# Orders of all engines from a list scheduler inside the kernel: a two-layer retention and attention trunk on one core

## The chip, the core and the metric

The kernel runs on one core of one Trainium2 chip. The metric is the device time of one execution in microseconds (us); lower is better. Below, PE is the matrix engine (TensorE), DVE the vector engine, ACT the scalar engine, POOL GpSimd, and SP the engine that issues most transfers (SyncE). Each engine works through its own list of instructions strictly in order; between engines there are only semaphores. So whatever stands late in one engine's list is late, even if its inputs have long been there.

## The reference, cut to what matters

A residual stream of 256 tokens by 2048 features goes through one retention layer and one latent-attention layer, each followed by a squared-ReLU MLP, all in float32:

```
x = x + retention(rms_norm(x), w_in, w_out, cos, sin)      # 8 heads, 2 chunks of 128 tokens
x = x + square(relu(rms_norm(x) @ w1[0])) @ w2[0]          # 2048 -> 8192 -> 2048
k_nope, k_pe, v = mla_shared_kv(rms_norm(x), w_kv_down, w_kv_up, ...)
x = x + mla_attention(rms_norm(x), w_dq, w_uq, w_o, k_nope, k_pe, v, cos, sin)   # 16 heads
x = x + square(relu(rms_norm(x) @ w1[1])) @ w2[1]
```

## The kernel before

**Precision and products.** Every large operand is split into a rounded high part and a low remainder: ACT writes the high part (`wh` for weights), DVE the remainder (`wl`), both in `split`. A product is three matmuls, high by high, high by low, low by high (lines 409 to 411 for most of the kernel).

**Tiling.** `gemm_pair` works through a 256-by-1024 block of weights ("quad") at a time and for some of the quads ("sevens", lists such as `SEVEN`, `ODD`, `LATE`) replaces eight block products by seven: DVE forms sums of weight blocks (`u`, lines 363, 372, 373), and sums of activation blocks were made ahead by `with_sums` (tiles named `..._more`). A plain quad costs PE 24 matmuls, a seven 21. Raw weights come into `raw` (3 buffers), split parts go to `wh` and `wl` (5 buffers each), other 2 KB tiles share `f2k` (14 buffers), activations `act` (24 buffers). PSUM has the tags `acc` (4 banks), `tp` (2) and `at` (one pair).

**Stages in order of time.** Retention: a first projection `rg`, then queries, keys and values (`rq`, `rk`, `rv`, `rp`) head by head, with short score and value products (`sc`, `o`) whose results `y` are transposed on PE and split; out-projection `ro`. MLP of layer 0: up-projections `u` and down-projections `d` alternate in four groups; hidden blocks are transposed on PE, squared and split into `hid` tiles. Then the new `x` is normed and transposed (`n_tp`) into `n` tiles; the key side `kd`, the query side `dqp`, `dq`; `ku`, `uq`; attention (`s`, `ptp`, `ao`) between pieces of `uq` and `wo`; the second MLP; stores.

**What sets the order.** The Python code decides it. `later(n, fn)` puts work off by a number of half-chunks of the weight stream, `tick` runs what is due, and the engines' lists follow the order of the calls as the framework schedules them. At some places `queued_behind` adds a dependency without a semaphore, to hold an instruction behind another one on its engine. Buffers of a tag are handed out in turn.

Of the kernel before, what the change touches and what calls it, by code (L numbers as in the profile page):

```python
# [14 lines left out]
I32 = mybir.dt.int32  # L15
AF = mybir.ActivationFunctionType
# [3 lines left out]


# [24 lines left out]
GROUPS = (4, 4, 4, 4)  # L46
SEVEN, LATE, ODD, HEAD = (3, 5, 7), (5, 7), (1, 3, 5, 7), (2, 4, 6, 7)
# [19 lines left out]
def yoco(ctx: ExitStack, tc: tile.TileContext, a):  # L67
    nc = tc.nc
# [3 lines left out]
    def f2k(shape, name, dtype=F32):  # L72
        return pool.tile([P, *shape], dtype, tag="f2k", bufs=14, name=name)

    def small(w, name):
        return pool.tile([P, w], F32, tag="small", bufs=36, name=name)
# [5 lines left out]
    def bank(tag, shape, name):  # L82
        t = psum.tile([P, 512], F32, tag=tag, bufs=4 if tag == "acc" else 2, name=name)
        return shaped(t, shape)

    def two_banks(name):
        return psum.tile([P, 2, 512], F32, tag="at", bufs=1, name=name)

    def act_tile(name, dtype=F32R):

        return pool.tile([P, 2, 2, S], dtype, tag="act", bufs=24, name=name)


    queue, low_part, first_low = [], [None], [None]
    clock, count, ahead = [0], itertools.count(), [None, None]
# [19 lines left out]
    gains = pool.tile([P, G_ALL], F32, name="gains")  # L115
    cst = pool.tile([P, C_ALL], F32, name="cst")
    pos_i = pool.tile([P, NT], I32, name="pos_i")
    gpe = pool.tile([P, 2 * ROPE], F32, name="gpe")
# [3 lines left out]
    neg_half = pool.tile([P, 16], F32, name="neg_half")  # L122
# [4 lines left out]
    zeros = pool.tile([P, 512], BF16, tag="junk", bufs=1, name="zeros")  # L127
# [6 lines left out]
    x_home = [[dram.tile([P, 512], F32, name=f"xh_{t}_{b}") for b in range(NB)] for t in range(NT)]  # L134
# [14 lines left out]
    def to_home(c, p):  # L149

        def send(t, j, i):
            ins = nc.gpsimd.dma_start(x_home[t][2 * p + j], c[t][j][i], accum_op=ALU.add)
            tc.add_manual_dep(
                ins.ins, low_part[0].ins.name,
                mybir.DependencyInfo(mybir.DependencyClass.Sync, mybir.DependencyReason.SCHED_ONLY), reason="spaced",
            )
# [8 lines left out]
    def sums_into_x(c, name):  # L165
# [6 lines left out]
        queued_behind(nc.vector.tensor_tensor(v, c["p6"], o["p1"], op=ALU.add), low_part[0])  # L172
        nc.vector.tensor_tensor(u, c["p7"], v, op=ALU.add)

        def join(*parts):
            for t, j, part, op in parts:
                queued_behind(nc.vector.tensor_tensor(x[t][j], x[t][j], part, op=op), low_part[0])
# [31 lines left out]
    def square_sum(src, acc, name):  # L209
        junk = pool.tile([P, 512], BF16, tag="junk", bufs=1, name=f"{name}_sq")  # L210
# [26 lines left out]

    def stream(w, chunk, cols, name, use, done=None, before=None):

        raw = pool.tile([P, 2048], F32, tag="raw", bufs=3, name=f"{name}_raw")  # L240
# [3 lines left out]
        for half in range(2):  # L244
            wh = pool.tile([P, 1024], F32R, tag="wh", bufs=5, name=f"{name}_wh{half}")
            wl = pool.tile([P, 1024], F32R, tag="wl", bufs=5, name=f"{name}_wl{half}")
# [10 lines left out]
            for i in range(cuts):  # L257
                lo = half * n + i * m
                low_part[0] = split(wh[:, i * m : (i + 1) * m], wl[:, i * m : (i + 1) * m], raw[:, lo : lo + m])
                if ahead[0] is not None:  # L260
                    queued_behind(low_part[0], ahead[0])
                    ahead[0] = None
# [52 lines left out]
    def queued_behind(ins, before):  # L315
        tc.add_manual_dep(
            ins.ins, before.ins.name,
            mybir.DependencyInfo(mybir.DependencyClass.NoSync, mybir.DependencyReason.DATA), reason="order",
        )

    def quad(w, chunk, x, mm, name, split_ends=False):

        raw = pool.tile([P, 2048], F32, tag="raw", bufs=3, name=f"{name}_raw")
# [9 lines left out]
        def parts(src, n, part, after=None):  # L333
            wh = pool.tile([P, 1024], F32R, tag="wh", bufs=5, name=f"{name}_wh{part}")
            wl = pool.tile([P, 1024], F32R, tag="wl", bufs=5, name=f"{name}_wl{part}")
            low = low_part[0] = split(wh[:, : n * 512], wl[:, : n * 512], src)
            if after is not None:
                queued_behind(low, after)
            if part == 0:
                first_low[0] = low  # L340
# [21 lines left out]
        u = [pool.tile([P, 2, 512], F32, tag="us", bufs=2, name=f"{name}_u{i}") for i in range(2)]  # L362
        first_sum = nc.vector.tensor_tensor(
# [3 lines left out]
        if first_low[0] is not None:  # L367
            queued_behind(first_sum, first_low[0])
        if ahead[1] is not None:
            queued_behind(first_sum, ahead[1])  # L370
            ahead[1] = None
        nc.vector.tensor_tensor(u[1][:, 0], u[0][:, 0], raw[:, 512:1024], op=ALU.add)
        summed_up = nc.vector.tensor_tensor(u[1][:, 1], u[1][:, 0], raw[:, 1536:], op=ALU.add)  # L373
        b11, b22 = parts(raw[:, 0:1024], 2, 0, summed_up)
        mm("p1", a(0, 0), b11)
        mm("c12", s(3), b22)
        (b21,) = parts(raw[:, 1536:], 1, 1, summed_up)
# [156 lines left out]
    def add_to_x(acc, b, ss, name):  # L534
        for t in range(NT):
            for part in acc[t] if isinstance(acc[t], tuple) else (acc[t],):
                added = nc.vector.tensor_tensor(x[t][b], part, x[t][b], op=ALU.add)
                if name == "n2" and b >= 2:
                    queued_behind(added, low_part[0])
# [19 lines left out]
    pos_f = pool.tile([P, NT], F32, name="pos_f")  # L559
# [733 lines left out]
```

## Time and profile before

| | |
|---|---|
| time, median of 3 runs | 2460.17 us (2459.62 to 2461.29) |
| span of the profiled execution, first to last instruction | 2456.3 us |
| median less span (the profiled execution's own total is not listed) | 3.9 us |
| busy share PE / PE weight loads / DVE / ACT / POOL | 100 / 84 / 90 / 67 / 10 % |
| granted TensorE clock | 1.000 |
| DMA mean | 212 GB/s |

A row of a timeline gives the start in us from the first instruction, the duration, the engine, line and operation, the tiles written and read, and in brackets the idle time before it with what ended it. A matmul's end in these rows is modelled: a 512-column matmul has 0.39 us, while its successor starts after 0.23 us. So time lost on PE is read from the distance between two starts, not from the idle time alone.

### The profile page before, as it was taken

The numbers are of one execution on the slowest core, as the hardware profiler recorded it, in microseconds if no ns is written. First come the engines' busy times: TensorE is split into PE (matmuls) and PEld (weight loads), VectorE is DVE, ScalarE is ACT, GpSimd is POOL, SyncE is SP. The second block draws the span as 40 slices with busy tenths as digits, with TensorE's granted clock in tenths as the row PEclk, the third lists the DMA queues.
The fourth block names the chain that finished last, engine by engine and source line by source line (L and its number), as shares of the span: only waits on it lengthen the run. The fifth ranks groups of instructions, "written<-read, shape, count | busy, mean of one in ns | idle before, by whom it ended". The sixth has DMA issues, their size and how long they took to land.

```text
span 2456.3 us, 31721 instructions
## 1 busy us (share of the span) xinstructions
PE 2446.2 (100%) x11614; PEld 2057.6 (84%) x11614; DVE 2212.2 (90%) x2919; ACT 1641.3 (67%) x2307; POOL 238.0 (10%) x287
## 2 busy tenths in 40 slices
PE   9999999999999999999999999999999999999999
PEld 7888888888888888888888888998888888888887
DVE  7899899888899999999999998777899999999998
ACT  6566666556676767667676777577667667676674
POOL 6400001000000010010110001101000100100100
PEclk9999999999999999999999999999999999999999
DMA  8555569556565586695786555444555865957854
GB/s 309 207 201 191 192 202 259 191 183 224 197 218 194 196 254 218 207 272 187 241 253 213 200 202 180 155 162 173 197 199 205 252 228 194 262 198 229 264 209 170
DMA packets 93692, 521.05 MB, mean 212 GB/s; under 512 B 11104, under 2 KB 12512, under 8 KB 40288
## 3 DMA queue, kind: packets, MB, share of 16 engines
q1 hardware_dynamic: 72144, 472.83, 55.2%
q0 software_dynamic: 21248, 46.15, 8.9%
q8 instruction: 91, 1.49, 0.2%
q14 instruction: 65, 0.53, 0.1%
q10 hardware_dynamic: 144, 0.05, 0.0%
HBM read 479.14 MB, written 39.85 MB: 211 GB/s over the span
## 4 chain that ended last, share of the span: by engine, by line
PE 92%; DVE 2%; ACT 1%; issue 0%; DMA 0%; POOL 0%; ACTq 0%; DVEq 0%
PE u_c L411 7%; PE u_c L410 7%; PE u_c L409 7%; PE d_c L411 6%; PE d_c L410 6%; PE d_c L409 6%; PE rp_c L411 3%; PE rp_c L409 3%; PE rp_c L410 3%; PE u_p L411 2%; PE u_p L410 2%; PE u_p L409 2%; PE rq_acc L307 2%; PE rk_acc L307 2%; PE ro_c L411 2%; PE ro_c L409 2%
## 5 line engine op out<-in xcount | busy, mean ns | idle before, releaser
L217 DVE TENSOR_TENSOR d_wl<-d_raw,d_wh 128x1024 fp32r<-128x1024 f32 (+1 forms) x256 | 278.7, 1111 | 31.6 <-ACT d_wh L216 31.6
L217 DVE TENSOR_TENSOR u_wl<-u_raw,u_wh 128x1024 fp32r<-128x1024 f32 (+1 forms) x256 | 279.3, 1113 | 29.8 <-ACT u_wh L216 29.8
L409 PE MATMUL u_c<-u_wh,n 128*128 128x512 f32 x712 | 278.3, 392 | 0.0
L411 PE MATMUL u_c<-u_wh,n 128*128 128x512 f32 x712 | 277.2, 389 | 0.0
L410 PE MATMUL u_c<-u_wl,n 128*128 128x512 f32 x712 | 277.2, 389 | 0.0
L409 PE MATMUL d_c<-d_wh,hid 128*128 128x512 f32 x706 | 275.4, 392 | 0.5 <-ACT d_wh L216 0.5
L411 PE MATMUL d_c<-d_wh,hid 128*128 128x512 f32 x706 | 275.0, 390 | 0.0
L410 PE MATMUL d_c<-d_wl,hid 128*128 128x512 f32 x706 | 274.8, 389 | 0.0
L216 ACT CAST u_wh<-u_raw 128x1024 fp32r<-128x1024 f32 (+1 forms) x256 | 241.3, 973 | 49.6 <-PE u_c L411 24.1
L216 ACT CAST d_wh<-d_raw 128x1024 fp32r<-128x1024 f32 (+1 forms) x256 | 240.3, 971 | 39.9 <-PE d_c L411 16.6
L216 ACT CAST d_wh<-d_u 128x1024 fp32r<-128x1024 f32 x106 | 108.1, 1051 | 119.7 <-DVE d_u L373 82.6
L216 ACT CAST u_wh<-u_u 128x1024 fp32r<-128x1024 f32 x104 | 106.2, 1052 | 116.0 <-DVE u_u L373 77.3
L411 PEld LDWEIGHTS u_c<-u_wh,n 128*128 128x128 f32 x712 | 133.7, 188 | 27.8
L410 PEld LDWEIGHTS u_c<-u_wl,n 128*128 128x128 f32 x712 | 133.8, 188 | 27.4 <-DVE u_wl L217 0.3
L409 PEld LDWEIGHTS u_c<-u_wh,n 128*128 128x128 f32 x712 | 133.7, 188 | 27.0
L409 PEld LDWEIGHTS d_c<-d_wh,hid 128*128 128x128 f32 x706 | 132.6, 188 | 28.2 <-ACT d_wh L216 1.4
L411 PEld LDWEIGHTS d_c<-d_wh,hid 128*128 128x128 f32 x706 | 132.5, 188 | 27.6
L410 PEld LDWEIGHTS d_c<-d_wl,hid 128*128 128x128 f32 x706 | 132.6, 188 | 27.5 <-DVE d_wl L217 0.4
L216 ACT CAST rp_wh<-rp_raw 128x1024 fp32r<-128x1024 f32 x112 | 103.8, 945 | 74.2 <-PE rp_c L411 49.2
L217 DVE TENSOR_TENSOR rp_wl<-rp_raw,rp_wh 128x1024 fp32r<-128x1024 f32 x112 | 119.7, 1090 | 16.4 <-ACT rp_wh L216 16.2
L217 DVE TENSOR_TENSOR u_wl<-u_u,u_wh 128x1024 fp32r<-128x1024 f32 x104 | 123.5, 1222 | 3.1 <-ACT u_wh L216 2.8
L217 DVE TENSOR_TENSOR d_wl<-d_u,d_wh 128x1024 fp32r<-128x1024 f32 x106 | 125.8, 1221 | 0.0
(570 smaller groups left out, 6505.3 us busy)
## 6 DMA issues: line engine op xcount, KB each, us to landing
u_raw<-in_mlp_w SPq DMA_DIRECT2D x128, 1024.0 KB, 5.4
d_raw<-in_mlp_w SPq DMA_DIRECT2D x128, 1024.0 KB, 4.9
rp_raw<-in_ret_w_gv SPq DMA_DIRECT2D x56, 1024.0 KB, 4.8
ro_raw<-in_ret_w_out SPq DMA_DIRECT2D x32, 1024.0 KB, 4.9
uq_raw<-in_mla_w_uq SPq DMA_DIRECT2D x24, 768.0 KB, 4.3
rq_raw<-in_ret_w_qk SPq DMA_DIRECT2D x16, 1024.0 KB, 4.9
rk_raw<-in_ret_w_qk SPq DMA_DIRECT2D x16, 1024.0 KB, 4.8
xh<-d_c POOLq DMA_DIRECT2D x48, 256.0 KB, 6.1
```

The lines of the kernel that those rows point to most:

```text
L216: nc.scalar.copy(h, src)
L217: return nc.vector.tensor_tensor(l, src, h.bitcast(F32), op=ALU.subtract)
L307: nc.tensor.matmul(acc[f], wh[:, cols], a.rearrange("p i s -> p (i s)"), start=k == 0, stop=k == nk - 1)
L409: nc.tensor.matmul(dst, ah, bh, start=n == 0, stop=False)
L410: nc.tensor.matmul(dst, ah, bl, start=False, stop=False)
L411: nc.tensor.matmul(dst, al, bh, start=False, stop=n == total[key] - 1)
```

## The change

All engine calls go to a `Plan` instead of the hardware queues. `record` notes each operation with the tiles it reads and writes (down to the single elements) and an estimated cost; nothing is emitted until the whole program is recorded. Then `due_dates` walks backwards and gives every operation a due time (the latest start by the costs of what follows it; PE's operations are chained in the recorded order), and `schedule` walks forward: on each engine, among the operations whose inputs and buffers are ready, the one with the earliest due time goes next. Buffers get a slot when an operation is placed, any free one, and for `f2k`, `act` and `small` not necessarily in turn. `emit` issues everything in that order, under a mode of the framework that keeps it.

With it `queued_behind` and all its uses go. Two more edits ride along: in the retention every transposed `y` block is now first copied by ACT from PSUM to SBUF and split from there (before, only the blocks that get sums; that is ten copies more), and in the MLP `with_sums` is recorded half a step after the split, which matters only to the recorded order. The code for turning blocks by DMA (`turn_by_dma`) is there but switched off by `TURNED_Y = 0` and `STEPS` of `None`. The lists of sevens are the same sets as before.

```diff
+AHEAD = {"f2k": 25000, "act": 30000, "small": 60000}
...
+class Plan:
+    LATENCY = {"PE": 55, "DVE": 36, "ACT": 48, "POOL": 110, "SP": 60}
...
+    def due_dates(self):
+        last = {}
+        for op in self.ops:
+            for other in op.before.values():
+                other.after.append((op, True))
+            if op.engine == "PE":
+                if "PE" in last:
+                    last["PE"].after.append((op, False))
+                last["PE"] = op
...
+        for op in reversed(self.ops):
+            op.due = 0.0
+            whole = op.took if op.moves is None else op.cost + sum(op.moves)
+            for other, finish in op.after:
+                gap = whole + self.LATENCY[other.engine] if finish and not (other.engine == op.engine == "PE") else op.cost
+                op.due = min(op.due, other.due - gap)
+            if not op.after:
+                op.due = -whole
...
+    def schedule(self):
...
+            best = None
+            for e in free:
+                w, r = waiting[e], ready[e]
+                while w and w[0][0] <= free[e]:
+                    _, _, op = heapq.heappop(w)
+                    heapq.heappush(r, (op.due, op.number, op))
+                at = free[e] if r else w[0][0] if w else None
+                if at is not None and (best is None or at < best[0]):
+                    best = (at, e)
...
+            op.start = at
+            free[e] = at + op.cost
+            if op.moves is None:
+                op.end = at + op.took
+            else:
+                server = max(server, at + op.cost) + op.moves[0]
+                op.end = server + op.moves[1]
...
+        order = self.schedule()
+        with self.tc.manual_schedule(engines=engines):
+            for op in order:
+                engine, method = op.method
+                fn = getattr(getattr(self.nc, engine), method)
+                op.made = fn(*(real(v) for v in op.args), **{k: real(v) for k, v in op.kw.items()})
...
-    nc = tc.nc
+    nc = Plan(tc.nc, tc)
...
-        if first_low[0] is not None:
-            queued_behind(first_sum, first_low[0])
...
+        def split_up(k2, src):
+            yt = act_tile(f"y{h}{k2}")
+            split_act(yt, src)
+            summed_up = len(y_act) in (HEAD if h < RH // 2 else LATE)
+            y_act.append((yt, with_sums(src, f"y{h}{k2}") if summed_up else None))
...
-                else:
-                    split_act(yt, tp)
+                u = f2k([2, S], f"yu{h}{k2}")
+                nc.scalar.copy(u, tp)
+                split_up(k2, u)
...
+                    if len(blocks) - 1 in ODD:
+                        later(0.5, lambda: entry.__setitem__(1, with_sums(u, name)))
```

**Three places in the engines' lists.** In the changed kernel all instructions carry line 421, the line that issues them. The order of PE is almost the one before; what moves is mostly DVE, ACT, SP and POOL.

SP, the start of the program, before (`x0t` is the transposed input, `rg_raw` the first weights, `cst` a table with the constants of the rotary angles, the mask and the identity for transposes):

```order
L648 DMA x0t_99<-in_xt 128x256
L253 DMA rg_raw<-in_ret_w_gv 128x512
L656 DMA x0t_99<-in_xt 128x256
L253 DMA rg_raw<-in_ret_w_gv 128x512 x2
...
L687 DMA pos_i<-in_pos 128x2
L688 DMA cst<-in_cst 128x672
```

SP, the same place with the change:

```order
L421 DMA cst<-in_cst 128x672
L421 DMA rg_raw<-in_ret_w_gv 128x512
L421 DMA x0t_77<-in_xt 128x256
L421 DMA rg_raw<-in_ret_w_gv 128x512
L421 DMA x0t_77<-in_xt 128x256
```

The table moves from the fourteenth place of the list to the first, ahead of all that the first matmul needs.

DVE, the end of the first MLP, before (`d_317` is the last quad of the last down-projection, `d_31_v`, `d_31_u` and `x_mlp` its sums into `x`, `kd` the first weights after it):

```order
L217 TENSOR_TENSOR d_317_wl_12571<-d_317_raw,d_317_wh_12570 128x1024
L177 TENSOR_TENSOR x_mlp_12025<-x_mlp_12025,d_31_u 128x512
L217 TENSOR_TENSOR d_317_wl_12587<-d_317_raw,d_317_wh_12586 128x1024
L177 TENSOR_TENSOR x_mlp_12106<-x_mlp_12106,d_31_p_12560 128x512 x2
L177 TENSOR_TENSOR x_mlp_12106<-x_mlp_12106,d_31_v 128x512
L177 TENSOR_TENSOR x_mlp_12106<-x_mlp_12106,d_31_u 128x512
L217 TENSOR_TENSOR kd_wl_12614<-kd_raw,kd_wh_12613 128x640
L537 TENSOR_TENSOR x_mlp_12025<-d_31_c_12209,x_mlp_12025 128x512
L537 TENSOR_TENSOR x_mlp_12025<-d_31_c_12213,x_mlp_12025 128x512
L217 TENSOR_TENSOR kd_wl_12638<-kd_raw,kd_wh_12637 128x640
```

DVE, the same place with the change:

```order
L421 TENSOR_TENSOR d_317_wl_12568<-d_317_raw,d_317_wh_12551 128x1024
L421 TENSOR_TENSOR d_317_wl_12581<-d_317_raw,d_317_wh_12557 128x1024
L421 TENSOR_TENSOR kd_wl_12590<-kd_raw,kd_wh_12565 128x640
L421 TENSOR_TENSOR kd_wl_12597<-kd_raw,kd_wh_12585 128x640
L421 TENSOR_TENSOR d_31_v<-d_31_p_12498,d_31_p_12574 128x512
L421 TENSOR_TENSOR x_mlp_11571<-x_mlp_11571,d_31_p_12574 128x512
L421 TENSOR_TENSOR d_31_u<-d_31_p_12498,d_31_v 128x512
L421 TENSOR_TENSOR kd_wl_12620<-kd_raw,kd_wh_12610 128x640
L421 TENSOR_TENSOR x_mlp_11571<-x_mlp_11571,d_31_u 128x512
L421 TENSOR_TENSOR x_mlp_11634<-x_mlp_11634,d_31_p_12578 128x512 x2
```

The remainders of the last weights, and of the first two pieces of `kd`, now stand ahead of the sums into `x`. In the last down-projection of the second MLP the same happens to its own weights.

DVE, the first down-projection of a group, before (`hid_13` is the last hidden block, `hid_13_more` its sums, `d_007` the weights of the quad that multiplies them):

```order
L217 TENSOR_TENSOR hid_13_7524<-hid_13_u,hid_13_7524 128x2x256
...
L217 TENSOR_TENSOR hid_13_more<-hid_13_sum,hid_13_more 128x2x256
...
L217 TENSOR_TENSOR d_006_wl_7712<-d_006_raw,d_006_wh_7711 128x1024
L372 TENSOR_TENSOR d_007_u_7730<-d_007_u_7729,d_007_raw 128x512
L373 TENSOR_TENSOR d_007_u_7730<-d_007_u_7730,d_007_raw 128x512
L217 TENSOR_TENSOR d_007_wl_7735<-d_007_raw,d_007_wh_7734 128x1024
```

DVE, the same place with the change:

```order
L421 TENSOR_TENSOR d_006_wl_7723<-d_006_raw,d_006_wh_7714 128x1024
L421 TENSOR_TENSOR d_007_wl_7732<-d_007_raw,d_007_wh_7720 128x1024
L421 TENSOR_TENSOR d_007_u_7705<-d_007_u_7705,d_007_raw 128x512
L421 TENSOR_TENSOR hid_13_7586<-hid_13_u,hid_13_7586 128x2x256
L421 TENSOR_TENSOR hid_13_more<-hid_13_sum,hid_13_more 128x2x256
L421 TENSOR_TENSOR d_007_wl_7754<-d_007_raw,d_007_wh_7728 128x512
```

The split of the last hidden block, and of its sums, moves from 22 and 16 rows ahead of the first remainder of `d_007` to two and three rows behind it.

More of the change, by code (lines that the diff above doesn't have):

```diff
@@ L802, in ret_valued @@
             vl = f2k([512], f"vl{h}{t}", F32R)
-            low = split(vh, vl, src[t], r0[t])
-            if ahead[0] is not None:
-                queued_behind(low, ahead[0])
+            split(vh, vl, src[t], r0[t])
             v.append((vh, vl))
@@ L895, in mlp @@
+                for i in range(2):
+                    later(TURNS[p % 2][i], lambda i=i: turn(i))
             for p in range(f0 // 2, (f0 + nf) // 2):
-                seven = SEVEN if p % 2 else ODD if p else LATE
+                seven = (ODD, SEVEN)[p % 2] if p else LATE
                 gemm_pair(
@@ L942, in yoco @@
     rc, ckv = [], []
[L943 removed]
+    kpe_t = nc.tile(pool, [P, 2, S], F32R, "kpe_t")
     def downed(acc, b):
```

524 lines of the change are left out of this document (428 added, 96 removed).

## The prediction

> **What bounds the kernel now.** I read the page's busy shares and chain first, then the busy time by stage, then the waits of PE and, at each place where PE waits, the timeline.
>
> The first row has the busy time and share of each engine, the second the engines' shares of the chain that ended last:
>
> ```profile
> PE 2446.2 (100%) x11614; PEld 2057.6 (84%) x11614; DVE 2212.2 (90%) x2919; ACT 1641.3 (67%) x2307; POOL 238.0 (10%) x287
> PE 92%; DVE 2%; ACT 1%; issue 0%; DMA 0%; POOL 0%; ACTq 0%; DVEq 0%
> ```
>
> PE is busy for all but 10.1 us of 2456.3, and it is the chain. No order makes the matmuls fewer, so a scheduler can win only what PE waits. Where that is, the stages tell (after the interval: busy time and count of PE, weight loads, DVE, ACT, POOL):
>
> ```profile
> 0.00:25.00 25.00, 22.88 (x87) 15.56 (x88) 16.64 (x30) 17.11 (x31) 6.83 (x11) 1.00 0.90 314
> 25.00:90.00 65.00, 64.89 (x340) 55.33 (x339) 49.18 (x58) 41.88 (x63) 37.24 (x30) 1.00 0.79 281
> 90.00:130.00 40.00, 38.89 (x187) 32.08 (x186) 36.97 (x53) 22.96 (x35) 20.44 (x29) 1.00 0.53 182
> 130.00:680.00 550.00, 550.00 (x2638) 461.97 (x2638) 497.95 (x633) 340.85 (x444) 31.89 (x53) 1.00 0.61 203
> 840.00:900.00 60.00, 60.00 (x267) 49.69 (x266) 54.88 (x61) 38.54 (x48) 7.82 (x9) 1.00 0.81 236
> 1340.00:1450.00 110.00, 108.66 (x572) 92.35 (x571) 100.48 (x161) 78.59 (x144) 8.43 (x11) 1.00 0.59 206
> 1740.00:2400.00 660.00, 660.00 (x2986) 547.96 (x2985) 617.51 (x736) 452.76 (x581) 50.55 (x61) 1.00 0.68 221
> 2400.00:2457.00 57.00, 51.29 (x224) 41.45 (x222) 49.99 (x60) 26.19 (x32) 0.00 (x0) 0.99 0.48 165
> ```
>
> From 130 to 680 us and through nearly all of both MLPs PE never idles. In the steady window 840 to 900 us it starts 267 matmuls in 60.00 us, one every 0.225 us, with DVE at 54.88 of 60. What there is to win lies at the start, at 90 to 130, at 1340 to 1450, and near the end.
>
> Since a matmul's modelled end overlaps its successor, an idle time understates the loss. These PE rows show the true one, as the distance of two starts less the normal one of 0.227 us (0.145 us for the 320-column `kd` and 0.11 us for `s`):
>
> ```profile
> 100.82 0.40 PE L409 MATMUL rp_c<-rp_wh,a 128*128 128x512 f32 x1
> 101.76 0.33 PE L235 MATMUL ytp<-cst,y 128*128 128x128 f32 x1 [0.54 <-DVE y L764]
> ...
> 112.72 0.39 PE L410 MATMUL rp_c<-rp_wl,a0s_more 128*128 128x512 f32 x1
> 113.67 0.45 PE L735 MATMUL sc<-rq_q,rk_q 128*128 128x256 f32 x1 [0.56 <-DVE y L217]
> ...
> 1374.79 0.39 PE L411 MATMUL d_c<-d_wh,hid 128*128 128x512 f32 x1
> 1375.64 0.63 PE L235 MATMUL n_tp<-cst,x_mlp 128*128 128x128 f32 x4 [0.46 <-DVE n L219]
> ...
> 1410.10 0.31 PE L280 MATMUL kd_acc<-kd_wl,n 128*128 128x320 f32 x1
> 1410.72 0.41 PE L281 MATMUL kd_acc<-kd_wh,n 128*128 128x320 f32 x1 [0.31 <-DVE n L219]
> ...
> 1685.92 0.28 PE L1127 MATMUL s<-kpe_t,qpe 128*128 128x128 f32 x1
> 1686.66 0.70 PE L1166 MATMUL ao<-pt,v 128*128 128x256 f32 x2 [0.46 <-ACT pt L1157]
> ...
> 2420.36 0.39 PE L409 MATMUL d_c<-d_wh,hid 128*128 128x512 f32 x1
> 2421.08 0.50 PE L409 MATMUL d_c<-d_wh,hid 128*128 128x512 f32 x1 [0.33 <-ACT d_wh L216]
> ...
> 2435.94 0.39 PE L409 MATMUL d_c<-d_wh,hid 128*128 128x512 f32 x1
> 2436.54 0.50 PE L409 MATMUL d_c<-d_wh,hid 128*128 128x512 f32 x1 [0.21 <-ACT d_wh L216]
> ```
>
> In this order: 0.71, 0.72, 0.62, 0.47, 0.63, 0.49, 0.37: 4.0 us in seven waits. The idle time gives 2.9 us for the same seven. The stages' idle time tells what these rows leave out: 1.34 us at 1340 to 1450, of which two waits above are 0.77, so as much again; beside it waits too short to be idle at all. I put all that an order can win after the start at 8 us: 4.0 in these rows and, by that ratio, about as much again in the smaller ones (an estimate).
>
> **Against which time.** The sum is made against the profiled execution: span 2456.3 us; its own total is not listed. The median of the runs is 2460.17, so 3.9 us lie around the span; I add every term to 2460.2.
>
> **Part 1, the constants first on SP: a loss.** The start before (issues on SP, then what PE waits for):
>
> ```profile
> 0.73 0.39 SPq L648 DMA_DIRECT2D x0t<-in_xt  x1
> 1.18 0.42 SPq L253 DMA_DIRECT2D rg_raw<-in_ret_w_gv  x1
> 4.22 0.62 ACT L216 CAST rg_wh<-rg_raw 128x512 fp32r<-128x512 f32 x1 [0.44 <-DMA rg_raw<-in_ret_w_gv]
> 4.89 1.00 PE L279 MATMUL rg_acc<-rg_wh,a 128*128 128x512 f32 x2
> 10.81 0.33 SPq L688 DMA_DIRECT2D cst<-in_cst  x1
> cst<-in_cst SPq DMA_DIRECT2D x1, 336.0 KB, 5.5
> 3.00:6.00 3.00, 3.00 (x10) 1.31 (x9) 1.59 (x4) 1.75 (x4) 0.00 (x0) 1.00 0.89 280
> ```
>
> PE's first real matmul waits for the cast of the first weights, and that for their transfer. Now 336 KB (344,000 bytes) go ahead of input and weights. At the 280 GB/s that the DMA moves from 3 to 6 us they take 1.2 us. The low bound is one issue slot, 1.18 - 0.73 = 0.45 us, if the transfers overlap. For the high bound I double the 1.2: the three last input tiles are now converted before the last weights of `rg`, and a second wait of that size may open there. I take 1.2: the DMA share of 0.90 in the first 25 us says that it is loaded, not waiting for issues. Nothing returns it: from 25 to 90 us PE idles 0.11 us of 65, so a late start stays a late start.
>
> **Part 2, POOL's long chain: nothing.** The rotary angles are worked out on POOL, and the change sets the eight stores of `x` and two small operations between its steps:
>
> ```profile
> 56.20 1.47 POOL L597 TENSOR_SCALAR tr_rr<-tr_rr 128x512 f32<-128x512 f32 x1
> 61.31 4.50 POOL L682 DMA_DIRECT2D xh<-x  x8
> ```
>
> The chain's end at 57.7 moves by at most the 4.5 us of the stores and some 2 of the two operations, to 64. On PE the transposes of the angles (`tr_tp`) move back by 25 matmuls, 25 x 0.227 = 5.7 us, so this lateness has its cover; if the cover is too short, `sc` at 84 us waits for the rest, up to 1 us.
>
> **Part 3, ten more copies on ACT: nothing.** A copy of 512 columns costs ACT 0.59 us at most:
>
> ```profile
> 2404.46 0.59 ACT L432 COPY d_c<-d_c 128x512 f32<-128x512 f32 x1 [1.61 <-PE d_c L411]
> ```
>
> Ten are 5.9 us, in stages where ACT works 340.85 of 550 us, and the blocks are used in `ro`, a whole head or more later. Without that slack they would cost at most these 5.9.
>
> **Part 4, the reordered DVE and ACT: a gain.** Of the waits above, those at 100 to 114 us are DVE behind its own row of sums and splits; with the weights' remainders spread among the rotations I take 1.0 of the 1.43 (between 0 and 1.43). At the end of the first MLP the remainders of `d_317` and of the first `kd` pieces go ahead of the sums into `x`; I take 2.3 of the some 3 lost at 1340 to 1450 (twice 1.34 with the overlap of ends added), since `n_tp` still needs the sum, its transpose and two splits in a row, which no order shortens (0 to 3). In the last down-projection the same move takes 0.6 of 0.86. In the attention the order of PE is the old one and its wait for `pt` is a chain over three engines: 0.3 of 0.63. Sum 4.2, bounds 0 and 8.
>
> **Part 5, new waits: a small loss.** Every moved row is late somewhere. In the MLPs the split of `hid_13` now stands behind the first remainder of `d_007`; at 54.88 of 60 us DVE has 8% to spare, and the buffers of `wl` let it run ahead. I take 0.3 in all; below nothing it cannot go, and its upper end is the slower rival.
>
> Sum: 2460.2 + 1.2 + 0 + 0 - 4.2 + 0.3 = 2457.5 us.
>
> **A rule that would promise far more.** The row of weight loads (busy time, mean ns, then the idle time before them):
>
> ```profile
> L411 PEld LDWEIGHTS u_c<-u_wh,n 128*128 128x128 f32 x712 | 133.7, 188 | 27.8
> ```
>
> The Trainium skill, "Perfetto Trace Analysis", "Identifying the Most-Contended Engine", says that matmul busy time does not show how near the roofline a kernel is, and to judge by the busy share of the weight loads. By that rule the 84% here leaves 16%, an estimate of 393 us, and the sum would be 2067 us. The trace is against its use here: 27.8 us over 712 loads are 39 ns before each, with no releaser named, and 188 + 39 is the start distance of 227 ns that holds where PE waits for nobody. A better order can't take these 39 ns.
>
> **The rivals.** (a) *All waits go*, because the scheduler knows each duration and places each row just in time: 2460.2 + 1.2 - 8 = 2453.4, or 2451.7 if the start costs only 0.45 and 1 us of its own waits goes too. For it: DVE idles in every one of these stages. Against: chains over three engines don't shorten. (b) *Slower: the hidden blocks come too late.* If DVE at `d_007` is less than two rows ahead of PE, then PE waits for the splits of `hid_13` and its sums, 0.60 us each by DVE's spacing, in each of eight groups: 8 x 1.2 = 9.6, less half the gain of part 4: 2460.2 + 1.2 + 9.6 - 2.1 = 2468.9. It decides as soon as DVE's lead there is under 1.2 us. Against it: DVE spends 54.88 of 60 us in that stage and PE waits nowhere. (c) *The waits only move*: the lists hold the same work, PE's order is nearly the same, and what is taken at one place is given back at the next; the start is paid: 2460.2 + 1.2 = 2461.4, up to 2463. (d) The rule above: some 2067 us.
>
> **How the numbers follow.** Forecast 0.50 (2457.5; its own range 2454.5 to 2460.5), (a) 0.22, (b) 0.12, (c) 0.15, (d) 0.01. The bound of 0.2%, 4.9 us, is about what a measurement of this kernel can tell from no change. Faster by more (under 2455.3): most of (a), a little of the forecast's lower side, and (d), 0.28. Slower by more (over 2465.1): (b) and a little of (c), 0.14. Within: 0.58. The range runs from 2452, near the lower end of (a), to 2465, which leaves out (b), (d) and a little of (c).
>
> **What the changed profile would show.** Right, if the first `rg` matmul starts at 6.1 us instead of 4.9; if the MLP stages still have no idle PE and about 267 matmuls in 60 us; if the waits of PE for `n`, `y` and `d_wh` shrink but for `n` stay; if POOL's chain ends near 64 us and PE does not wait for `tr_tp`. Wrong, if PE shows `hid_13` or `hid_more` as what it waits for, if ACT or DVE waits for a raw weight transfer that comes later than before, or if the first 25 us lose more than 2 us.

## The result: 39.4 us slower, with PE idle no longer than before

The time went from 2460.73 us (median of 4 runs, 2459.62 to 2462.70) to 2500.10 us (4 runs, 2499.03 to 2502.80). The ratio is 1.0162, 95% interval 1.0148 to 1.0176. The forecast was 2457.5 with a range of 2452 to 2465: wrong, and on the other side.

Engines and chain on the page of the changed kernel:

```profile
PE 2490.9 (100%) x11614; PEld 2061.5 (82%) x11614; DVE 2218.2 (89%) x2919; ACT 1645.5 (66%) x2317; POOL 242.4 (10%) x287
PE 96%; DMA 2%; DVE 2%; ACT 0%; issue 0%; SPq 0%; ACTq 0%; DVEq 0%
```

The same 11614 matmuls keep PE "busy" for 44.7 us more than before (2446.2), and PE has more of the chain, not less. The loss is not waiting: PE is idle for 10.1 us of the span in both traces (2456.3 less 2446.2 before, 2501.0 less 2490.9 now). These are all the places after 130 us at which PE waits for another engine (total, times, longest); they sum to 2.4 us, as in the trace before:

```profile
PE rp_p L421 <- DVE rp_wl L421: 1.3, 1, 1.3
PE n_tp L421 <- ACT n2u L421: 0.5, 1, 0.5
PE o L421 <- DVE vl L421: 0.4, 1, 0.4
PE rp_c L421 <- DVE rp_wl L421: 0.2, 1, 0.2
```

The stages, in the form of the prediction (interval, then busy time and count of PE, weight loads, DVE, ACT, POOL, granted clock, DMA share, GB/s):

```profile
25.00:90.00 65.00, 64.40 (x331) 54.43 (x330) 43.74 (x53) 40.64 (x59) 45.81 (x34) 1.00 0.80 285
90.00:130.00 40.00, 39.84 (x195) 32.97 (x194) 37.51 (x56) 24.96 (x38) 20.62 (x29) 1.00 0.50 179
840.00:900.00 60.00, 60.00 (x260) 48.38 (x259) 56.68 (x65) 37.48 (x44) 5.43 (x7) 1.00 0.69 217
1740.00:2400.00 660.00, 660.00 (x2925) 536.36 (x2924) 601.22 (x713) 439.17 (x572) 50.86 (x65) 1.00 0.68 217
```

The third row is the finding. PE is busy for all of the 60 us, at a granted clock of 1.00, and starts 260 matmuls where it started 267. In the fourth it is 2925 for 2986. The time from one matmul to the next has become longer, and a busy time can't show that. The row of weight loads says it again (busy time, mean ns, idle time before):

```profile
L421 PEld LDWEIGHTS u_c<-u_wh,n 128*128 128x128 f32 x1424 | 267.5, 188 | 61.7
```

A load still takes 188 ns, but 61.7 us over 1424 loads are 43 ns before each; before, the same loads stood in two rows with 27.8 and 27.0 us over 712 each, 38 to 39 ns. Taken from all starts in the two traces that lie less than 0.3 us apart, the distance between two 512-column matmuls is 227.0 ns before (8762 of them) and 232.1 ns after (8759): 8759 x 5.15 ns = 45.1 us. With the other shapes and the changes between shapes it is 44 us.

The rest is seen when the n-th matmul of one trace is set against the n-th of another. The table gives by how many us PE is later than in the kernel before, each time counted from the first instruction of its own trace, at places named by the time before; the last three columns are kernels of the experiments below, two of them with the lists of the changed kernel, word for word:

```
place (us before)      changed   e1_small_apart   e8 (e1 again)   e7_rp_lands_later
  25  rg                  2.5          1.4              0.9                2.0
  50  rk                  2.4          1.3              0.8                1.9
  90  rk                  3.4          2.1              1.7                2.7
 130  rp                  2.7          0.9              0.5                1.6
 400  rp                  6.4          0.9              0.4                1.8
 420  rp_p                9.0          3.4              0.8                1.8
 680  ro                 13.1          3.4              1.4                1.5
1340  d, layer 0         28.2          3.5              1.5                1.6
1450  dqp                26.6          0.5             -1.5               -1.4
1740  wop                29.6         -0.1             -2.2               -2.1
2400  d, layer 1         44.8         -0.1             -2.2               -2.1
2450  d, layer 1         44.8         -1.3             -3.3               -3.2
```

In the first column the lag grows by 15 us from 680 to 1340 and by 15 us again from 1740 to 2400, in the MLPs, where the trace has no wait of PE that could grow. Where a stretch has fewer 512-column matmuls, as in the attention (1450 to 1740), it grows by less.

The traces overstate the difference of the medians, 44.7 against 39.4. The profiled execution of the changed kernel has a total of 2502.8 for a span of 2501.0; 1.8 us lie around the span, not the 3.9 that the prediction took from a median. So the profiled execution of the kernel before stands for some 2458, a fast one, and that of the changed kernel is its slowest.

### The profile page after: what moved, and what is told of

It reads as the page before. It is cut to its first block, busy times and chain, and to the rows that moved or that the text cites. A ratio compares the mean times of both kernels' runs of the same rounds, so it can differ in the third digit from the quotient of the medians.

```text
span 2501.0 us, 31752 instructions
## 1 busy us (share of the span) xinstructions
PE 2490.9 (100%) x11614; PEld 2061.5 (82%) x11614; DVE 2218.2 (89%) x2919; ACT 1645.5 (66%) x2317; POOL 242.4 (10%) x287
## 4 chain that ended last, share of the span: by engine, by line
PE 96%; DMA 2%; DVE 2%; ACT 0%; issue 0%; SPq 0%; ACTq 0%; DVEq 0%
PE u_c L421 21%; PE d_c L421 21%; PE rp_c L421 8%; PE d_p L421 6%; PE u_p L421 6%; PE ro_c L421 4%; PE uq_acc L421 4%; PE rk_acc L421 3%; PE rq_acc L421 3%; PE rp_p L421 3%; PE ku_acc L421 2%; PE wo_acc L421 2%; PE wop_c L421 1%; PE dqp_c L421 1%; PE hid_tp L421 1%; PE rg_acc L421 1%
## 5 line engine op out<-in xcount | busy, mean ns | idle before, releaser
L421 PE MATMUL u_c<-u_wh,n 128*128 128x512 f32 x1424 | 467.4, 395 | 0.0
L421 PE MATMUL d_c<-d_wh,hid 128*128 128x512 f32 x1412 | 464.2, 395 | 0.0
L421 PEld LDWEIGHTS u_c<-u_wh,n 128*128 128x128 f32 x1424 | 267.5, 188 | 61.7
L421 PE MATMUL rp_c<-rp_wh,a 128*128 128x512 f32 x560 | 183.5, 394 | 0.0
L421 DVE TENSOR_TENSOR u_wl<-u_u,u_wh 128x1024 fp32r<-128x1024 f32 x104 | 126.6, 1222 | 27.8 <-ACT u_wh L421 27.6
L421 PEld LDWEIGHTS rp_c<-rp_wh,a 128*128 128x128 f32 x560 | 105.1, 188 | 23.9
L421 PE MATMUL ro_c<-ro_wh,y 128*128 128x512 f32 x368 | 120.1, 396 | 0.0
L421 POOL DMA_DIRECT2D xh<-d_c x48 | 41.6, 867 | 775.0 <-DVE d_wl L421 444.2
```

What stands on the lines that cost most here:

```text
L421: op.made = fn(*(real(v) for v in op.args), **{k: real(v) for k, v in op.kw.items()})
```

## What else the change did: every slot of a buffer got a tag of its own

The placement of tiles is in one line of the change that the prediction passed over:

```diff
-        return pool.tile([P, *shape], dtype, tag="f2k", bufs=14, name=name)
...
+            kw = dict(tag=f"{tag}{buf.slot}", bufs=1) if tag else {}
+            return pool.tile(shape, dtype, name=name, **kw)
```

Before, the 14 slots of `f2k`, the 5 of `wh` and so on lie in a row each. Now each slot is placed where it is first used, with the small tiles (4 to 32 bytes a partition, 32 bytes of room) between the large ones. By the addresses in the built programs, every slot of `wh`, `wl`, `act`, `f2k` and `raw` before starts at 192 modulo 256 bytes. After, `wh` and `wl` start at 32 or 64, and the 24 slots of `act` at 0 (2), 32 (2), 64 (6), 96 (6), 128 (1) and 192 (7). A matmul reads one tile as moving rows and one as weights. Here are the 512-column matmuls of the changed kernel that are followed by one with the same two places, sorted by the distance of weights and rows, with the start distances from the trace:

```
weights less moving rows, modulo 256     matmuls    mean ns to the next start
   0                                       1504        228.7   (median 227)
  32                                       1990        233.0
  64                                       1044        233.1
  96                                        101        233.6
 128                                       1322        233.0
 160                                        803        233.7
 192                                        324        229.5
 224                                        737        233.3
```

Only where the two lie at the same place modulo 256 is the old 227 ns the usual value. That is a correlation; the experiments make it a cause.

## The experiments

**e0_table: the cadence alone, by where the operands lie.** Two tiles, and slices of them that start at chosen bytes:

```python
for s in sorted(w):                                       # wa .. wh: 0, 32, .. 224
    stage(f"w{chr(97 + s // 32)}_m", [(w[s], m[0]), (v[s], m[0])])
for s in (32, 64, 128):                                   # bothb, bothc, bothe
    stage(f"both{chr(97 + s // 32)}", [(w[s], m[s]), (v[s], m[s])])
stage("own", [(w[0], m[0]), (w[32], m[32])])
stage("next", [(w[0], m[32]), (w[32], m[0])])
```

> This kernel leaves the whole computation out: it only runs stages of 160 matmuls each on constant operands, alternating between two weight tiles, with nothing else at work. The stages differ in where the weights lie against the moving rows, counted in bytes modulo 256 (wa to wh: 0, 32, ... 224), in where both lie together (bothb, bothc, bothe: both shifted by 32, 64, 128), in which neighbour is shifted (own: weights match the moving rows of their own matmul and miss those of the matmul before by 32; next: the other way round), and in length (nc: 384 columns, nb: 256). Theory (the relative place of the two operands sets the cadence): wa and the three both stages run at 0.227 us for one matmul of 512 columns, so 36.3 us for 160; wb to wh run at 0.231 to 0.235, so 37.0 to 37.6. Of own and next one is slow and one is fast, if only one neighbour counts. Rival 1 (the new lists, their waits and counters slow PE): all stages at 36.3. Rival 2 (a start that is 32 bytes off a multiple of 64 is slow by itself): wb, wd, wf, wh and bothb slow, wc, we, wg and the other both stages fast.

PE's timeline has a row for each stage (start, duration to the modelled end of its last matmul):

```profile
40.39 36.44 PE L32 MATMUL acc_wa_m<-mv,wt 128*128 128x512 f32 x160
76.66 37.49 PE L32 MATMUL acc_wb_m<-mv,wt 128*128 128x512 f32 x160
113.99 37.50 PE L32 MATMUL acc_wc_m<-mv,wt 128*128 128x512 f32 x160
151.32 37.64 PE L32 MATMUL acc_wd_m<-mv,wt 128*128 128x512 f32 x160
188.80 37.35 PE L32 MATMUL acc_we_m<-mv,wt 128*128 128x512 f32 x160
...
263.31 36.79 PE L32 MATMUL acc_wg_m<-mv,wt 128*128 128x512 f32 x160
299.94 37.49 PE L32 MATMUL acc_wh_m<-mv,wt 128*128 128x512 f32 x160
337.28 36.46 PE L32 MATMUL acc_bothb<-mv,wt 128*128 128x512 f32 x160
...
446.18 37.23 PE L32 MATMUL acc_own<-mv,wt 128*128 128x512 f32 x160
483.25 36.98 PE L32 MATMUL acc_next<-mv,wt 128*128 128x512 f32 x160
520.08 27.90 PE L32 MATMUL acc_nc_wa<-mv,wt 128*128 128x384 f32 x160
547.81 27.90 PE L32 MATMUL acc_nc_wb<-mv,wt 128*128 128x384 f32 x160
```

From one start to the next, over 160: `wa` 36.27 us or 226.7 ns, `wb` 37.33 or 233.3, `wd` 234.3, `we` 232.4, `wg` (192 bytes) 228.9. With nothing but PE at work the stages come within 0.8 ns of the table of the changed kernel in seven of its eight classes (distance 0 has 226.7 here, a mean of 228.7 and a median of 227 there): no list, wait or other engine is needed. Moving both operands (`bothb`) costs nothing, so it is the distance and not the start. Missed: of `own` and `next` I expected one to be fast; both are slow, at 231.7 and 230.2, less than when both miss (233.3), which fits weights that have to match the rows of their own matmul and of the neighbour; no run separates the two further. At 384 columns 32 bytes cost nothing (173.3 both), which fits that 545 such matmuls in the kernel lost only 1 ns each. At 256 columns they cost nothing either (120.0 at 0 bytes, 118.3 at 32).

**e9_table_two: smaller and larger distances, and bf16.** The same stages with other slices.

> This kernel leaves the whole computation out: stages of 160 matmuls on constant operands with nothing else at work, as in e0_table. sa to si: fp32r, the weights lie 0, 4, 8, 16, 32, 256, 288, 384, 512 bytes beside the moving rows, modulo nothing. halfa to halfg: bf16, which lies 128, 144, 160, 192, 0, 64, 128 bytes apart modulo 256. Theory (what counts is the distance modulo 256): sa, sf and si take 36.3 to 36.5 us, se and sg 37.5 as the 32-byte stage did, sh 37.35 as the 128-byte stage did; 4, 8 and 16 bytes are open, between 36.3 and 37.5. For bf16, which reads half the bytes, an effect of at most the same size, with halfe the fastest. Rival (the period is longer than 256 bytes): sf or sg differ from the stages of e0_table, or si does.

```profile
41.13 36.44 PE L33 MATMUL acc_sa<-mv,wt 128*128 128x512 f32 x160
77.41 37.35 PE L33 MATMUL acc_sb<-mv,wt 128*128 128x512 f32 x160
...
151.51 37.49 PE L33 MATMUL acc_sd<-mv,wt 128*128 128x512 f32 x160
...
226.16 36.46 PE L33 MATMUL acc_sf<-mv,wt 128*128 128x512 f32 x160
262.46 37.49 PE L33 MATMUL acc_sg<-mv,wt 128*128 128x512 f32 x160
299.79 37.35 PE L33 MATMUL acc_sh<-mv,wt 128*128 128x512 f32 x160
336.98 36.44 PE L33 MATMUL acc_si<-mv,wt 128*128 128x512 f32 x160
373.26 34.71 PE L33 MATMUL acc_halfa<-hv,ht 128*128 128x512 bf16 x160
...
511.40 34.70 PE L33 MATMUL acc_halfe<-hv,ht 128*128 128x512 bf16 x160
```

256 and 512 bytes (`sf`, `si`) are as good as 0, while 288 and 384 (`sg`, `sh`) cost what 32 and 128 do: the period is 256. One element of 4 bytes (`sb`) costs nearly as much as any other distance. In bf16 the distance costs nothing; all seven stages take 34.5 us, 215.9 ns for a matmul.

**e1_small_apart: the changed kernel, only the addresses changed.** The small tiles and constants get a pool of their own:

```diff
+    few = ctx.enter_context(tc.tile_pool(name="few", bufs=1))
     pool = ctx.enter_context(tc.tile_pool(name="sb", bufs=1))
...
-        return nc.tile(pool, [P, w], F32, name, "small", 36)
+        return nc.tile(few, [P, w], F32, name, "small", 36)
...
-    gains = nc.tile(pool, [P, G_ALL], F32, "gains")
+    gains = nc.tile(few, [P, G_ALL], F32, "gains")
```

(and the same for `cst`, `pos_i`, `gpe`, `neg_half`, `pos_f`, `gqn`). All tiles of 2 KB and more in `pool` then start at 192 modulo 256; each engine's list is unchanged.

> The changed kernel with its small tiles and constants in a pool of their own; the lists of all engines are word for word the same, only the addresses differ: weights, activations and blocks now all start at the same place modulo 256 bytes. Theory: the cadence goes back to 0.227 us, all 44 us of it come back, and what stays is the later start (+2.5) less the waits that the scheduler took away (-2.2): 2461, between 2456 and 2465. Rival 1 (lists and counters): 2500, no change. Rival 2 (starts 32 bytes off a multiple of 64): 2461 as well.

Measured: 2456.82 us (11 runs) against 2460.19, ratio 0.9988, interval 0.9979 to 0.9996; inside the expected range, 4 us below its middle. The stage of the finding:

```profile
840.00:900.00 60.00, 60.00 (x267) 49.69 (x266) 56.17 (x62) 40.05 (x49) 7.82 (x9) 1.00 0.77 235
```

267 again. Addresses alone carry more than the whole loss, 43 us by the medians. The lists themselves are worth about 3 us, by the interval 1 to 5.

**e2_gap_32 and e3_all_by_32: the kernel before, only the addresses changed.** One unused tile of 32 bytes; in e2 it is set between the weight tiles and the activations, in e3 ahead of all large tiles:

```diff
e2                                              e3
+        if not c:                              +    pool.tile([P, 8], F32, name="gap")
+            pool.tile([P, 8], F32, name="gap")      x0t_0 = f2k([2, S], "x0t_0")
         v = act_tile(f"a0_{c}")
```

> The kernel before with one unused tile of 32 bytes a partition set between the weight tiles and the activation tiles; nothing else differs. Theory: every matmul of 512 columns has its two operands 32 bytes apart and takes 0.233 instead of 0.227 us: 8700 x 6 ns = 52 us more by the profile, 46 if the timed runs show it as after the change: 2506 to 2515. Rival 1 (lists and counters): 2461, no change. Rival 2 (starts 32 bytes off a multiple of 64): slower too, as the activations now start there.

> The kernel before with the same unused 32 bytes ahead of all large tiles, so that every one of them moves by 32 bytes and none against another. Theory: no change, 2461, between 2458 and 2464. Rival 1 (lists and counters): no change either. Rival 2 (starts 32 bytes off a multiple of 64): both operands now start there, slower by 40 us or more.

e2 took 2509.90 us, ratio 1.0204 (1.0189 to 1.0220): one tile that nobody reads costs 50 us. e3 took 2459.83, ratio 0.9997 (0.9988 to 1.0006). The MLP stage of e2, then of e3:

```profile
840.00:900.00 60.00, 60.00 (x259) 48.29 (x258) 55.14 (x59) 35.85 (x42) 6.09 (x7) 1.00 0.73 222
```

```profile
840.00:900.00 60.00, 60.00 (x267) 49.69 (x266) 54.95 (x61) 38.71 (x48) 7.82 (x9) 1.00 0.81 243
```

Rival 1, the new lists with their waits and counters, falls with e1 and e2. Rival 2, starts off a multiple of 64, falls with e3, `bothb` and `wc`.

**e5_before_cst_first: the first part of the prediction by itself.**

```diff
+    nc.sync.dma_start(cst, a["cst"])
     x0t_0 = f2k([2, S], "x0t_0")
...
-            nc.sync.dma_start(cst, a["cst"])
```

> The kernel before with the transfer of the constants issued first on SP; nothing else is moved. Theory: the first rg matmul comes 1.2 us or more late, PE runs a stretch of matmuls at 0.427 us if the gap ahead of it is long enough, and the total rises by 1.2 to 2.7 us: 2462.5. Rival (made good before the end): 2460.2.

Measured: 2460.71 against 2459.95, ratio 1.0004 (0.9995 to 1.0012), that is -1.2 to +3.0 us; it doesn't tell the two apart. In its trace PE starts late, and slowly (matmuls 0.43 us apart, a granted clock of 0.61 from 7.9 to 9.5 us), and the 3.3 us that it is late at 50 us are 3.6 at 2450. This execution is 1 us above the median of its runs:

```profile
7.93 0.97 PE L279 MATMUL rg_acc<-rg_wh,a 128*128 128x512 f32 x2 [2.84 <-ACT rg_wh L216]
8.69 0.76 PE L280 MATMUL rg_acc<-rg_wl,a 128*128 128x512 f32 x1
9.24 0.63 PE L281 MATMUL rg_acc<-rg_wh,a 128*128 128x512 f32 x1
```

**e4_slots_free: why the constants went first.** At time 0 the scheduler charges a buffer slot that nobody has used 60 ns on SP. The constants need no such slot, so they alone were ready, and a ready operation goes first however late it is due. One condition mends it, on top of e1:

```diff
-                late = max(late, slots[t][0][0] + self.LATENCY[op.engine])
+                if slots[t][0][0]:
+                    late = max(late, slots[t][0][0] + self.LATENCY[op.engine])
```

> The kernel with the small tiles apart, and one line of the scheduler mended: a buffer that has never been used is free at once, not 60 ns late. At time 0 the constants were the only transfer on SP that needs no such buffer, and so went first; now they stand at place 19, beside the positions. Theory (the constants ahead of the first weights cost the start, and the gap lets PE's clock fall back): the first rg matmul starts near 4.9 us, without a stretch of matmuls at 0.427 us, and the total falls by 1.6 (seven matmuls fewer by 25 us in the profile) to 2.7: 2454.5, between 2453 and 2456. Rival (the late start is made good later, or the angles' chain on POOL, which starts at the same time as before this edit, sets the end of the stage): no change, 2456.8.

Measured: 2457.94 against 2459.95, ratio 0.9994 (0.9985 to 1.0003), and the first matmul of `rg` starts where it did before the change, without a stretch of matmuls 0.43 us apart:

```profile
4.82 0.50 PE L422 MATMUL rg_acc<-rg_wh,a 128*128 128x512 f32 x1
5.16 0.47 PE L422 MATMUL rg_acc<-rg_wl,a 128*128 128x512 f32 x1
```

The expected 1.6 to 2.7 us did not come. By 25 us PE stands 1.0 us later than before the change, against 1.4 and 0.9 in the two traces of e1's program: waits for the next weights and inputs take most of the start back, which speaks for the rival. Its lists are those of e1 after the first 90 us, but its trace then loses 3.2 us at 400 to 420 us and 1.8 in the 100 us ahead of it, where e1 loses nothing; that can't come from the edit.

**e6_later_landing: the longest new wait, by a table number.** In the trace of e1 PE waits 1.71 us at 405.71, and the lists show why. First PE, then DVE, then the transfers between 380 and 410 us (KB each, median us to landing):

```profile
405.71 0.50 PE L421 MATMUL rp_p<-rp_wl,a0s_more 128*128 128x512 f32 x1 [1.71 <-DVE rp_wl L421]
```

```profile
399.30 0.69 DVE L421 TENSOR_TENSOR ro_p<-ro_p,ro_u 128x512 f32<-128x512 f32 x1
403.29 1.23 DVE L421 TENSOR_TENSOR rp_u<-rp_raw 128x1024 f32<-128x1024 f32 x1 [3.30 <-DMA rp_raw<-in_ret_w_gv]
404.44 1.22 DVE L421 TENSOR_TENSOR rp_wl<-rp_u,rp_wh 128x1024 fp32r<-128x1024 f32 x1
```

```profile
rp_raw<-in_ret_w_gv SPq DMA_DIRECT2D x5, 1024.0 KB, 8.7
```

DVE stands before the sums of the next block, whose raw weights are 8.7 us on the way, while the split behind them (`rp_wl<-rp_u`), which PE needs, has its inputs. The scheduler's table has 0.38 + 3.0 + 1.8 = 5.2 us for such a transfer, and in an order made by it the sums come at the right time. So I changed the number, on top of e4:

```diff
-            rate, wait = ... else (349, 3000 if engine == "POOL" else 1800)
+            rate, wait = ... else (349, 3000 if engine == "POOL" else 4000)
```

> The kernel of the run e4_slots_free with one number of the scheduler's table changed: a transfer from SP is taken to land 4.0 us after its bytes are through instead of 1.8 (1 MB in 7.4 us instead of 5.2). Theory (the one long new wait of PE, 1.7 us at rp_p, is there because the sums of the next block stand ahead of a split whose input was ready, and wait 3.3 us on DVE for a transfer that took 8.7 us): the splits go first, that wait is gone, and the total is 1 to 2 us below the run e4_slots_free. Rival (any such number only moves the waits): the same time within 1 us, with a wait of over 0.5 us in another place.

Measured: 2461.78 against 2459.95, ratio 1.0006 (0.9997 to 1.0014). The wait at `rp_p` is gone, and others took its place; between 900 and 1340 us, where e1 has none:

```profile
PE u_c L422 <- DVE u_wl L422: 2.7, 3, 1.0
```

The rival was right that the waits only move. Neither time came: by the medians 2461.78 is 3.8 us above e4 (2457.94), where 1 to 2 us below it or the same within 1 us was expected.

**e7_rp_lands_later, with e8_small_apart_again beside it.** The later landing for the `rp` stages alone, on top of e1:

```diff
+            if engine == "SP" and any(isinstance(v, View) and v.buf.name.startswith("rp") for v in outs):
+                wait = 4000
```

> The kernel of the run e1_small_apart (small tiles apart) with the later landing, 4.0 us instead of 1.8 after the bytes are through, for the weights of the rp stages alone, where the longest new wait stands. From the end of those stages on the lists stay as in e1_small_apart. Theory (that wait is an order made for a transfer that lands earlier than it does): the wait of 1.7 us for the split at rp_p goes, the 2.6 us that e1_small_apart lost against the kernel before at 400 to 420 us fall to under 1, and the total is 2455, between 2453.5 and 2456.5. Rival (the waits only move, as they did in e6_later_landing): 2456.8 or more, with a new wait of over 0.5 us in an rp stage.

> The kernel of the run e1_small_apart once more, beside e7_rp_lands_later on the same chip: 2456.8, between 2455 and 2458.5, faster than the kernel before by 3 us.

e7 took 2455.21 us against 2459.95, ratio 0.9983 (0.9974 to 0.9992), its 11 runs between 2454.34 and 2456.81. e8, which is e1's program again, took 2457.7 (ten runs, 2454.78 to 2460.41; an eleventh, of 3050.56, is not in the median), ratio 0.9990 (0.9981 to 0.9999); e1 had run between 2454.30 and 2461.31. In e7 DVE does the splits ahead of the sums, waits less, and PE doesn't wait at `rp_p`:

```profile
398.72 2.36 DVE L423 TENSOR_TENSOR rp_wl<-rp_u,rp_wh 128x1024 fp32r<-128x1024 f32 x2
400.99 0.68 DVE L423 TENSOR_TENSOR ro_p<-ro_p,ro_u 128x512 f32<-128x512 f32 x1
402.54 1.23 DVE L423 TENSOR_TENSOR rp_u<-rp_raw 128x1024 f32<-128x1024 f32 x1 [0.86 <-DMA rp_raw<-in_ret_w_gv]
```

The trace of e8 has the lists of e1 and no wait there: the raw weights took 6.9 us to land (median from 383 to 412 us) against 8.1 in e1, and the sums ran at 400.45 without waiting. So this wait is not in the order alone; it opened in the execution where the transfer was late. In e7's trace the landing took 7.0 us, near e8's, so the trace doesn't show that its order is safe at 8.1; that its 11 runs spread over 2.5 us, where those of e1 and e8 spread over 7.0 and 5.6, speaks for it. The expected time came, though part of the fall against e1 is that executions differ; against e8, on the same chip, it is 2.5 us.

**e10_both: e7 with the condition of e4.**

> The kernel of the run e7_rp_lands_later with the one line of e4_slots_free (a buffer never used is free at once, so that the constants are issued at place 19). Theory of the start (the transfers set the pace of the first 25 us, whoever goes first): 2455.2, within 1 us of e7_rp_lands_later. Rival (the start as first matmul and clock show it): 1.3 us less, 2453.9.

2455.39 us against 2459.55, ratio 0.9980 (0.9971 to 0.9989): the same as e7 within 0.2 us. In the two traces the first `rg` matmul comes 1.1 us earlier (4.97 for 6.06), and at 25 us nothing of it is left (2.3 us late, for 2.0). e7 and e10 are faster than both kernels, by 4 to 5 us against the one before and by 45 against the changed one.

## Why the prediction was wrong, step by step

**The step that failed** is the first: "No order makes the matmuls fewer, so a scheduler can win only what PE waits", with 0.227 us as the fixed distance of two starts and "about 267 matmuls in 60 us" as the sign of it. It was 260. The distance depends on where the two operands lie, and the change moves the tiles against each other. The sum has no term for placement; that term is +44 us by the traces, +43 by the medians of e1 and the changed kernel. The range could not hold it either, since none of the rivals had it.

**Part 1, the start: +1.2 taken, bounds 0.45 and 2.4.** In the changed kernel PE is 2.5 us late at 25 us, with its lists and good addresses 0.9 to 2.0. The first `rg` matmul came at 6.61, not 6.1 (5.54 to 6.26 in e1, e7 and e8):

```profile
6.61 1.22 PE L421 MATMUL rg_acc<-rg_wh,a 128*128 128x512 f32 x2 [1.40 <-ACT a L421]
7.62 0.63 PE L421 MATMUL rg_acc<-rg_wl,a 128*128 128x512 f32 x1
8.05 0.63 PE L421 MATMUL rg_acc<-rg_wh,a 128*128 128x512 f32 x1
8.48 0.63 PE L421 MATMUL rg_acc<-rg_wl,a 128*128 128x512 f32 x1
```

What the term did not have is a slow stretch: from 6.61 to about 13 us the matmuls of this trace start every 0.43 us, PE at about half its pace. In e5, with the same 0.43 us, the clock records show a granted clock of 0.5 from 8.3 to 11.7 us; here they begin only at 12.8 us, and the 1.00 in the row of a window before that has no record behind it. The idle time ahead of the first matmul doesn't decide it: e8, with the same lists, has 1.61 us there, more than the 1.40 here, and starts its matmuls 0.23 us apart after the first two. So 2.5 us belongs to this execution, and why it was slow there stays open. Some of the start is made good within 25 us, as e10 shows. The term was right in sign, and with good addresses its 1.2 lies within the 0.9 to 2.0.

**Part 2, POOL's chain: end at 64, cost nothing, or "up to 1 us" without cover.** The end moved by 14.7 us instead of 6, to 72.4 (start 71.74, 0.62 long). Its first step needs the positions, which SP now issues at 15.33 us instead of 10.13, and starts at 22.77 instead of 18.1; the rest came between its steps, where the stores now stand. The cover was too short by a little:

```profile
74.52 0.44 PE L421 MATMUL tr_tp<-cst,tr_scaled 128*128 128x128 f32 x2 [0.60 <-DVE tr_scaled L421]
```

Between 50 and 90 us the lists lose 0.8 to 0.9 us in e1, e7 and e8. The bound held, the value taken did not.

**Part 3, ten copies: nothing.** No run takes them out alone. PE waits for no `y` in any trace that has the new lists; in the trace before it did twice, 0.5 and 0.6 us.

**Part 4, waits that go: -4.2 taken, bounds 0 and -8.** By the table, on e8: -1.2 from 90 to 130 us (1.0 taken), -3.0 from 1340 to 1450 (2.3), -0.7 in the attention (0.3), -1.1 in the last down-projection (0.6). The sum is -5.9 before rounding: each of the four was right in place and sign and somewhat too small. No run changes one of these orders alone, so the causes that the prediction names for the single waits stay argued.

**Part 5, new waits: +0.3 taken.** 0.9 in e8 between 400 and 680 us and 2.6 in e1, all in the retention layer, where the term put them in the MLPs. The slower rival (b) did not occur: `hid_13` and `d_007` are not among the waits.

**The sum without the missing term** was nearly right: the lists alone give 2456.8 and 2457.7 in e1 and e8, against 2457.5. Part of that is luck: waits that went by 1.7 us more than taken stand against losses at POOL's chain and in the retention layer that were taken as 0 and 0.3 (0.8 and 0.9 in e8). And it is no credit to the forecast, which was for the whole change.

**Rival (d).** The busy share of the loads fell from 84 to 82% while the kernel became slower, because a load of 188 ns fills less of a longer start distance. So it moved the right way, where the busy share of the matmuls stayed at 100%; it is the 393 us that it promised which nothing here bears out. Where the prediction says that "a better order can't take these 39 ns", it should have asked what sets them: 5 ns more of them came with the addresses.

## What to carry to other kernels

Count the matmuls that start in a fixed window of a stage in which PE never waits, before and after: the busy share of the matmuls, the waits and the clock all stayed the same here while a matmul took 2% longer on average. Whatever changes how tiles are allocated (tags, slots, pools, the order of first use) can change addresses; for fp32r matmuls of 512 columns keep the moving and the weight tiles at the same place modulo 256 bytes, by giving small tiles a pool of their own. And read the whole diff as a change: a scheduler was announced, but the line with the 44 us was the one that names the tags.

## What was new about the hardware

- An fp32r matmul of 512 columns starts every 226.7 ns when its weights and its moving rows, and those of the neighbour, lie at the same place modulo 256 bytes, and every 229 to 234 ns when they don't, 4 bytes included. At 384 columns 32 bytes cost nothing and 128 bytes 2.7 ns; at 256 columns 32 bytes cost nothing. The stages ran with no other engine at work, so none has a part in it; by which mechanism PE loses the time, no run here shows. The Trainium skill, "SBUF — State Buffer", "Operand start alignment", gives a multiple of the element size as the rule for an operand's start and calls that legality, not speed; all these starts ran, and the runs put a price on them.
- In bf16 the distance has no price: 215.9 ns in all seven stages. The Trainium skill, "TensorE: Matmul & The Clock Gate", "Wait — 56ns, not 53.3ns?", has 215.7 ns for back-to-back matmuls of 512 columns on a warm array and 426.7 on a cold one. The bf16 stages agree with the first, and the 0.43 us between fp32r matmuls in e5, where the granted clock is 0.5, with the second; at full clock fp32r is 11 ns above it even with the best placement.
- Two executions of one program differ by 1.2 us in how long 1 MB of weights takes to land (8.1 against 6.9 us, median over the same stretch), and in the one PE waits 1.7 us at that place, in the other not at all. A difference of one wait between two single traces is not yet a difference of two kernels.
